# GpSimd's multiplies and adds of the even mixer and of three norms, moved to VectorE in a two-layer diffusion step

## The chip, the cores and the metric

The kernel runs on one core of one Trainium2 chip. Its time is the device time of one execution in microseconds (us). The engines are named as in the profile: PE is TensorE (matrix products), DVE is VectorE, ACT is ScalarE, POOL is GpSimd, SP issues the DMAs. Each engine works through a queue of its own in order, and an instruction at the head of a queue that waits for another engine holds up all behind it.

## The reference, cut to what matters

Two layers over 128 context and 512 latent tokens (640 columns in all), 1024 features. Layer 0 mixes with pooling and a short convolution, layer 1 with attention; each is followed by a SwiGLU block, and each of these sub-layers begins with an RMS norm.

```python
def rms_norm(x, g):
    return x * rsqrt(mean(x * x, -1) + EPS) * g
def window_mean(x, w):            # centred, w = 2, 4, 8, 16 for the four groups of 128 features
    return (cs[hi] - cs[lo]) / cnt
def pool_mixer(u, w_grp, scale):  # per group
    return einsum(window_mean(ug, w) - ug, w_grp) * scale
def short_conv_mixer(bg, cg, v, conv_w, conv_b):
    z = cg * v
    conv = sum(zp[:, k:k+L] * conv_w[k] for k in range(3)) + conv_b
    return bg * conv
def even_mixer(h, ...):
    u, bg, cg, v = split(h @ w_in)
    return concat([pool_mixer(u), short_conv_mixer(bg, cg, v)]) @ w_out
```

## The kernel before, in words

Activations lie transposed: 128 features on the partitions, the 640 tokens in the columns, so the 1024 features are eight blocks. All numbers are 32-bit. A product of two 32-bit matrices is made of three passes of PE: each operand is split into a high part (made by ACT, line 142) and the rest (a subtraction, line 143, on DVE). Names that begin with `wh`/`wl` are the two parts of a weight, `ah`/`al` and `bh`/`bl` those of an activation. A weight block of 128 output features takes 48 matmuls of 320 columns.

**The even mixer.** `project("pi", ...)` makes 16 blocks of the input product `pi`: four for pooling, then for each of four `j` the blocks c, v and b of the convolution. A block is taken out of PSUM by DVE (`ev`, line 505), and its shift column by ACT (line 510); three PSUM tiles go round, so PE can begin block n+3 only when block n has been taken out, and the small products `py` of the pooling take tiles from the same three. `pool_branch` builds the window sums by doubling: one add for width 2, two for 4, three for 8, four for 16, all on POOL (line 878). `conv_sum` multiplies c and v (line 935, POOL, after ACT has added the shift to c) and adds the two outer taps (line 958, POOL; ACT makes the scaled copies, line 957); for `j = 3` the same is done by DVE alone (lines 939 and 960). Then `project("po", ...)` makes the eight blocks of the output product.

**Beside it** DVE computes the modulation rows of both layers, which belong to no block: `ada.run` (line 365, `junk`) multiplies a 1024-wide row by the conditioning vector in halves of 512 with a sum. They are pinned into DVE's queue in program order, some in each block; between them a scheduler places the other instructions by its own estimates when the program is built, so the order in a queue is fixed before the run.

**The norms.** `updater` makes what follows each output block: the residual (three DVE instructions, line 490), `prep` (the next product's operand: `ah` by ACT, line 467, `al` by DVE, line 469) and `nrm.add`, the square by ACT (line 422) and its addition to the sum `ssq` by POOL (line 424, seven per norm). It serves three norms: `a1` after the even mixer, `b0` after layer 0's SwiGLU, `b1` after attention. `finish` splits the sum (lines 142 and 143) and PE adds it over the partitions (`ms`, line 453), one block into the next product `fi`.

Of the kernel before, what the change touches and what calls it, by code (L numbers as in the profile page):

```python
# [11 lines left out]
AF = mybir.ActivationFunctionType  # L12
ALU = mybir.AluOpType
# [4 lines left out]
KB = D // P  # L18
CTX = 128
LAT = 512  # L20
T = CTX + LAT
# [37 lines left out]
def hybrid_step(  # L59
# [23 lines left out]
    V, S, G, PE = nc.vector, nc.scalar, nc.gpsimd, nc.tensor  # L83
# [18 lines left out]
    def tmp(name):  # L102
        return tpool.tile([P, UL], F32, tag="t", name=name)

    x = pers.tile([P, KB, T], F32, name="x")
# [30 lines left out]
    def bias(ev, cond):  # L136
        return ev[:, T + cond : T + cond + 1]
# [8 lines left out]
    class Pipe:  # L146


        def __init__(self):
            self.due, self.now = [], 0  # L150
# [35 lines left out]
    class Stream:  # L186
# [7 lines left out]
        eng = V  # L194
# [213 lines left out]
    class Norm:  # L408
        def __init__(self, name):
            self.name = name  # L410
            self.acc = tmp(f"ssq_{name}")
            self.n = 0

        def add(self, k, eng=None, cols=slice(0, T), pool_only=False):
            if pool_only and k > 1:
# [13 lines left out]
    def log_exp_tables():  # L429
        tc.keep_in_program_order(S.preload_act_table_set("natural_log_exp_and_others"))  # L430
# [31 lines left out]
    def prep(k, dst, l, n):  # L462
        assert (l, 3 * n + 1, 4 if (l, 3 * n + 1, 4) in known and k < 4 else 8) in known
        h, lo = dst
        s = sc[l, n]
        for c, a, b in SEG:
            S.activation(h[:, k, a:b], x[:, k, a:b], AF.Identity, scale=s[:, k, c : c + 1])  # L467
        for c, a, b in SEG:
            V.scalar_tensor_tensor(  # L469
                out=lo[:, k, a:b],  # L470
                in0=x[:, k, a:b],
                scalar=s[:, k, c : c + 1],
                in1=h[:, k, a:b].bitcast(F32),
                op0=ALU.mult,
                op1=ALU.subtract,
            )

    def prep_shift(dst, l, n):
        assert (l, 3 * n, 8) in known
        h, lo = dst  # L480
        sh = mod[l][:, 24 * n : 24 * n + 8, :]
        V.tensor_copy(h[:, :, T:TX], sh)
        V.tensor_tensor(out=lo[:, :, T:TX], in0=sh, in1=h[:, :, T:TX].bitcast(F32), op=ALU.subtract)

    def update(m, l, gate0, parts):

        assert (l, gate0 // 8, 8) in known
        for c, a, b, got in parts:
            xs = x[:, m, a:b]
            V.scalar_tensor_tensor(  # L490
                out=xs,
                in0=got[:, 0 : b - a],
                scalar=mod[l][:, gate0 + m, c : c + 1],
                in1=xs,
                op0=ALU.mult,
                op1=ALU.add,
            )

    def residual(ps, m, l, gate0):
        parts = ((0, 0, CTX, ps[:, 0]), (1, CTX, HT, ps[:, 0, CTX:]), (1, HT, T, ps[:, 1]))  # L500
        update(m, l, gate0, parts)
# [11 lines left out]
    def shifted(ev):  # L513
        for c, a, b in SEG:
            S.activation(ev[:, a:b], ev[:, a:b], AF.Identity, bias=bias(ev, c))
        return ev
# [29 lines left out]
    def updater(l, gate0, nrm, then):  # L546
        def done(k, ps):
            residual(ps, k, l, gate0)
            prep(k, *then)
            nrm.add(k)  # L550
            if k == KB - 1:
                prep_shift(*then)
                log_exp_tables()
                pipe.later(1, lambda: [nrm.finish(span) for span in ((0, HT), (HT, T))])

        return done
# [167 lines left out]
    with tc.tile_pool(name="pool1", bufs=1) as p1:  # L724
# [41 lines left out]
        nrm = Norm("a0")  # L766
# [85 lines left out]
        def seqs(pad):  # L852
            return ((0, pad, CTX), (1, 2 * pad + CTX, LAT))
# [11 lines left out]
        def pool_branch(g, ev):  # L865
            up = tmp(f"up_{g}")
            for z in (0, PAD + CTX, 2 * PAD + T):
                G.memset(up[:, z : z + PAD], 0.0)
            for c, o, n in seqs(PAD):
                a = c * CTX  # L870
                S.activation(up[:, o : o + n], ev[:, a : a + n], AF.Identity, bias=bias(ev, c))
            w, cur, lo, hi = 1, up, 0, UL
            while w < WINDOWS[g]:
                nxt = tmp(f"s_{g}_{w}")
                q = w // 2
                lo, hi = (lo + 1, hi) if w == 1 else (lo + q, hi - q)
                back, on = (1, 0) if w == 1 else (q, q)
                G.tensor_tensor(
                    out=nxt[:, lo:hi], in0=cur[:, lo - back : hi - back], in1=cur[:, lo + on : hi + on], op=ALU.add
                )  # L880
                w, cur = 2 * w, nxt
            pipe.later(2, lambda: pool_mid(g, up, cur))

        def pool_mid(g, up, cur):
            pl = tmp(f"pl_{g}")
            for c, o, n in seqs(PAD):
                e = ends(cur, o, n, PAD)
                V.tensor_tensor(out=e, in0=e, in1=edge(g)[:, c], op=ALU.mult)
                V.scalar_tensor_tensor(
                    out=pl[:, c * CTX : c * CTX + n],  # L890
                    in0=cur[:, o : o + n],
                    scalar=1.0 / WINDOWS[g],
                    in1=up[:, o : o + n],
                    op0=ALU.mult,
                    op1=ALU.subtract,
                )
            plp = tuple(t[:, (5, 6, 4, 5)[g], 0:T] for t in bufB)
            pair(plp, pl[:, 0:T])
            pipe.later(3, lambda: pool_end(g, plp))
# [23 lines left out]
        ZL = T + 3  # L923

        def conv_sum(j, evc, evv):

            z = tmp(f"z_{j}")
            for o in (0, CTX + 1, ZL - 1):
                G.memset(z[:, o : o + 1], 0.0)
            if j < 3:  # L930
                shifted(evc)
            for c, o, n in seqs(1):
                a = c * CTX
                if j < 3:
                    G.tensor_tensor(
                        out=z[:, o : o + n], in0=evc[:, a : a + n], in1=evv[:, a : a + n], op=ALU.mult
                    )
                else:
                    V.scalar_tensor_tensor(
                        out=z[:, o : o + n],  # L940
                        in0=evc[:, a : a + n],
                        scalar=bias(evc, c),
                        in1=evv[:, a : a + n],
                        op0=ALU.add,
                        op1=ALU.mult,
                    )
            cvt = tmp(f"cv_{j}")

            def cw(i):
                return sm[:, S_CW + 4 * i + j : S_CW + 4 * i + j + 1]  # L950

            inner = slice(1, ZL - 1)
            S.activation(cvt[:, inner], z[:, inner], AF.Identity, scale=cw(1), bias=sm[:, S_CB + j : S_CB + j + 1])
            for i, d, t in ((0, -1, evc), (2, 1, evv)):
                zd = z[:, 1 + d : ZL - 1 + d]
                if j < 3:
                    S.activation(t[:, inner], zd, AF.Copy, scale=cw(i))
                    G.tensor_tensor(out=cvt[:, inner], in0=cvt[:, inner], in1=t[:, inner], op=ALU.add)
                else:
                    V.scalar_tensor_tensor(  # L960
                        out=cvt[:, inner], in0=zd, scalar=cw(i), in1=cvt[:, inner], op0=ALU.mult, op1=ALU.add
                    )
            return cvt

        def conv_gate(j, evb, cvt):
# [15 lines left out]
        def mixer_in(i, ev):  # L981
            if i < 4:
                return pool_branch(i, ev)
            j, what = divmod(i - 4, 3)
            if what == 0:
                evs["c"] = ev
            elif what == 1:
                evs["z"] = conv_sum(j, evs["c"], shifted(ev))
            else:
                cvt = evs["z"]  # L990
                if j < 3:
                    pipe.later(1, lambda: conv_gate(j, ev, cvt))
                else:
                    conv_gate(j, ev, cvt)
# [560 lines left out]
```

## Time and profile before

| | |
|---|---|
| time, median of 3 runs | 1409.69 us (1408.79 to 1410.60) |
| the profiled execution's own time | 1408.83 us |
| its span in the profile | 1406.9 us, 22549 instructions |
| PE, busy share of the span | 97% |
| DVE, busy share | 72% |
| ACT, busy share | 41% |
| POOL, busy share | 11% |
| mean granted PE clock | 0.983 of full speed |

The span runs from the first to the last instruction; the execution's own time holds 1.9 us more. The shares are averages over stages that differ: DVE is busy nine tenths or more in the slices from 70 to about 245 us, six to eight tenths of them from there to 600 us, and less on the whole after that. An instruction's duration counts its queueing for memory too, so the same form can be long in one place and short in another.

### The profile page before, as it was taken

The page shows a single profiled execution, that of the slowest core. Times are in us where ns is not written, and L with a number is a line of the kernel's source. Part 1 is how long each engine was busy: PE and PEld are TensorE (multiplying, and loading weights), DVE is VectorE, ACT ScalarE, POOL GpSimd, SP SyncE. Part 2 cuts the span into 40 slices and gives each one's busy share as a digit, 9 for nine tenths or more (in the row PEclk, how much of TensorE's full clock was granted, in tenths as well). Part 3 has the DMA queues.
Part 4 walks back from the last instruction along what each step waited for, and adds up shares of the span by engine and source line. Part 5 has one row for each costly group of instructions (what it writes and reads, how often), then busy time and mean ns, then how long its engine had stood idle before and what let it go on. Part 6 is the DMA issues. An engine that isn't in the chain of part 4 may idle for free.

```text
span 1406.9 us, 22549 instructions
## 1 busy us (share of the span) xinstructions
PE 1361.5 (97%) x9139; PEld 1332.9 (95%) x9139; DVE 1006.5 (72%) x1955; ACT 578.1 (41%) x1025; POOL 148.4 (11%) x116
## 2 busy tenths in 40 slices
PE   6989998999999999999999999999999999999995
PEld 3889998999999999999999899999999999999995
DVE  4899999777768787754667677778973477536745
ACT  3433334332112221232465676547652255414543
POOL 3351112000000000000203221020000000000003
PEclk7999999999999999999999999999999999999998
DMA  9634544434343534221232111012132122311212
GB/s 363 248 106 153 184 150 157 152 135 165 135 165 122 176 123 168 87 90 46 91 110 93 46 46 39 31 44 77 41 111 91 32 89 90 121 61 61 76 46 75
DMA packets 36728, 154.50 MB, mean 110 GB/s; under 512 B 3984, under 2 KB 11152, under 8 KB 26000
## 3 DMA queue, kind: packets, MB, share of 16 engines
q1 hardware_dynamic: 36624, 153.07, 31.2%
q8 instruction: 71, 1.16, 0.3%
q14 instruction: 33, 0.27, 0.1%
HBM read 147.55 MB, written 2.88 MB: 107 GB/s over the span
## 4 chain that ended last, share of the span: by engine, by line
PE 78%; DVE 16%; issue 2%; ACT 2%; DMA 1%; POOL 1%; SPq 0%; DVEq 0%; POOLq 0%; ACTq 0%
PE fi L287 26%; PE fo L287 21%; PE fi L610 16%; DVE junk L365 6%; PE pq L287 5%; PE wa L287 2%; DVE al L469 2%; PE o L1289 2%; PE s L1239 1%; DVE wl_in L143 1%; PE t L1272 1%; DVE x L490 1%; DVE wl_out L143 1%; DVE bl L143 1%; DMA raw_ada<-wada 1%
## 5 line engine op out<-in xcount | busy, mean ns | idle before, releaser
L365 DVE CUSTOM_DVE_ANT_0 junk<-rawa,silb 128x512 f32<-128x512 f32 x336 | 250.5, 746 | 7.6 <-ACT silb L793 1.0
L287 PE MATMUL fi<-al,wh_fi 128*128 128x320 f32 x832 | 192.2, 312 | 2.2 <-DVE al L469 2.2
L287 PE MATMUL fi<-ah,wh_fi 128*128 128x320 f32 x832 | 192.5, 313 | 1.4 <-ACT ah L467 1.4
L287 PE MATMUL fi<-ah,wl_fi 128*128 128x320 f32 x832 | 191.6, 312 | 0.0
L490 DVE SCALAR_TENSOR_TENSOR x<-fo,mod,x 128x128 f32<-128x128 f32 (+1 forms) x144 | 54.6, 433 | 136.5 <-PE fo L287 133.1
L287 PEld LDWEIGHTS fi<-al,wh_fi 128*128 128x128 f32 x832 | 141.7, 190 | 2.8 <-DVE al L469 2.8
L287 PEld LDWEIGHTS fi<-ah,wh_fi 128*128 128x128 f32 x832 | 141.7, 191 | 1.6 <-ACT ah L467 1.6
L287 PEld LDWEIGHTS fi<-ah,wl_fi 128*128 128x128 f32 x832 | 141.4, 190 | 0.0
L142 ACT ACTIVATE wh_fi<-raw_fi 128x1024 fp32r<-128x1024 f32 x52 | 55.0, 1058 | 172.0 <-PE fi L287 134.8
L142 ACT ACTIVATE wh_fi_p<-raw_fi 128x512 fp32r<-128x512 f32 x126 | 77.3, 627 | 111.8 <-PE fi L610 65.0
L142 ACT ACTIVATE wh_fo<-raw_fo 128x1024 fp32r<-128x1024 f32 (+1 forms) x48 | 47.5, 991 | 180.5 <-PE fo L287 132.6
L143 DVE TENSOR_TENSOR wl_fi_p<-raw_fi,wh_fi_p 128x512 fp32r<-128x512 f32 x126 | 85.6, 688 | 48.5 <-ACT wh_fi_p L142 48.2
L610 PE MATMUL fi<-bh,wl_fi_p 128*128 128x320 f32 x288 | 88.9, 309 | 0.0
L610 PE MATMUL fi<-bh,wh_fi_p 128*128 128x320 f32 x288 | 88.7, 308 | 0.0
L610 PE MATMUL fi<-bl,wh_fi_p 128*128 128x320 f32 x288 | 88.3, 307 | 0.0
L287 PE MATMUL fo<-bh,wh_fo 128*128 128x320 f32 x352 | 80.6, 310 | 0.0
L287 PE MATMUL fo<-bh,wl_fo 128*128 128x320 f32 x352 | 80.5, 310 | 0.0
L287 PE MATMUL fo<-bl,wh_fo 128*128 128x320 f32 x352 | 80.4, 310 | 0.0
L424 POOL TENSOR_TENSOR ssq_b<-ssq_b,sq_b 128x640 f32<-128x640 f32 x14 | 25.2, 1801 | 516.6 <-ACT sq_b L422 516.5
L287 PE MATMUL fo<-al,wh_fo 128*128 128x320 f32 x328 | 75.1, 310 | 0.0
L287 PE MATMUL fo<-ah,wh_fo 128*128 128x320 f32 x328 | 74.9, 309 | 0.0
L287 PE MATMUL fo<-ah,wl_fo 128*128 128x320 f32 x328 | 74.8, 309 | 0.0
(342 smaller groups left out, 3317.1 us busy)
## 6 DMA issues: line engine op xcount, KB each, us to landing
raw_fi<-wfi SPq DMA_DIRECT2D x44, 1024.0 KB, 4.8
rawa<-wada SPq DMA_DIRECT2D x84, 512.0 KB, 3.5
raw_fo<-wfo SPq DMA_DIRECT2D x16, 1024.0 KB, 4.9
raw_ada<-wada SPq DMA_DIRECT2D x12, 512.0 KB, 9.3
raw_in<-win SPq DMA_DIRECT2D x6, 1024.0 KB, 6.4
raw_fo<-wfo SPq DMA_DIRECT2D x8, 768.0 KB, 4.2
raw_qkv<-wqkv SPq DMA_DIRECT2D x6, 1024.0 KB, 4.8
raw_out<-wout SPq DMA_DIRECT2D x4, 1024.0 KB, 4.8
```

What stands on the lines that cost most here:

```text
L142: S.activation(h, src, AF.Copy)
L143: eng.tensor_tensor(out=l, in0=src, in1=h.bitcast(F32), op=ALU.subtract)
L287: PE.matmul(ps[:, h, 0 : hi - lo], w[a][:, k, cols], rhs[b][:, k0 + k, lo:hi], start=k == 0 and a == b, stop=k == kn - 1 and a == 1,)
L365: op = V.tensor_tensor_reduce(out=junk, in0=raw[:, cols], in1=silb[:, c, cols], scale=1.0, scalar=0.0, op0=ALU.mult, op1=ALU.add, accum_ou ...
L424: (eng or G).tensor_tensor(out=self.acc[:, cols], in0=self.acc[:, cols], in1=sq[:, cols], op=ALU.add)
L469: V.scalar_tensor_tensor(out=lo[:, k, a:b], in0=x[:, k, a:b], scalar=s[:, k, c : c + 1], in1=h[:, k, a:b].bitcast(F32), op0=ALU.mult, op1= ...
L490: V.scalar_tensor_tensor(out=xs, in0=got[:, 0 : b - a], scalar=mod[l][:, gate0 + m, c : c + 1], in1=xs, op0=ALU.mult, op1=ALU.add,)
L610: PE.matmul(out, w[a][:, k, :], ops.get(OPERAND[p], b)[:, k, :], start=fresh and k == 0 and a == b, stop=k == ops.kn - 1 and a == 1, skip_ ...
L1239: PE.matmul(self.ps[:, hf, 0:HT], bufB[a][:, self.h, q0 : q0 + P], kt[b][:, self.kv, hf * HT : hf * HT + HT], start=n == 0, stop=n == 2,)
L1272: PE.transpose(flat(pt)[:, s * P : s * P + P], self.pe[:, s * P : s * P + P], ident)
L1289: PE.matmul(po[:, 0 : 2 * P], vt[a][:, self.kv, s * P : s * P + P], got[b][:, s, :], start=s == 0 and n == 0, stop=s == 4 and n == 2,)
```

## The change

Every POOL multiply and add named above goes to DVE: the ten window sums; the three products c·v with the shift as the instruction's scalar operand, so that ACT's shift of c goes; the six outer taps as one multiply-add each, so that ACT's scaled copies go. `Norm` gets `square` and `add_square`: the square is made ahead of `prep`, and the addition is put behind `prep` and one block late, on DVE. `Norm.add` stays for the first and the last norm.

```diff
+        def square(self, k):
+            sq = tmp(f"sq_{self.name}_{k}") if k else self.acc
+            S.activation(sq[:, 0:T], x[:, k, :], AF.Square)
+            self.waiting.append(sq)
+
+        def add_square(self, eng):
+            sq = self.waiting.pop(0)
+            if sq is not self.acc:
+                eng.tensor_tensor(out=self.acc[:, 0:T], in0=self.acc[:, 0:T], in1=sq[:, 0:T], op=ALU.add)
...
             residual(ps, k, l, gate0)
+            nrm.square(k)
             prep(k, *then)
-            nrm.add(k)
+            if k:
+                nrm.add_square(V)
+            if k == KB - 1:
+                nrm.add_square(V)
...
-                G.tensor_tensor(
+                V.tensor_tensor(
                     out=nxt[:, lo:hi], in0=cur[:, lo - back : hi - back], in1=cur[:, lo + on : hi + on], op=ALU.add
                 )
...
-            if j < 3:
-                shifted(evc)
             for c, o, n in seqs(1):
                 a = c * CTX
-                if j < 3:
-                    G.tensor_tensor(
-                        out=z[:, o : o + n], in0=evc[:, a : a + n], in1=evv[:, a : a + n], op=ALU.mult
-                    )
-                else:
-                    V.scalar_tensor_tensor(
...
+                V.scalar_tensor_tensor(
+                    out=z[:, o : o + n],
+                    in0=evc[:, a : a + n],
+                    scalar=bias(evc, c),
+                    in1=evv[:, a : a + n],
+                    op0=ALU.add,
+                    op1=ALU.mult,
+                )
...
-                if j < 3:
-                    S.activation(t[:, inner], zd, AF.Copy, scale=cw(i))
-                    G.tensor_tensor(out=cvt[:, inner], in0=cvt[:, inner], in1=t[:, inner], op=ALU.add)
-                else:
-                    V.scalar_tensor_tensor(
...
+                V.scalar_tensor_tensor(
+                    out=cvt[:, inner],
+                    in0=z[:, 1 + d : ZL - 1 + d],
+                    scalar=cw(i),
+                    in1=cvt[:, inner],
+                    op0=ALU.mult,
+                    op1=ALU.add,
+                )
```

The scheduler orders the queues anew. The first place is DVE's queue where the pooling begins, from the first part of the weight split `wl_in_0_546` (`s` are window sums, `pl` the pooled result, `kc` the edge factors). Before:

```order
L143 TENSOR_TENSOR wl_in_0_546<-raw_in_138,wh_in_0_545 128x1024
L888 TENSOR_TENSOR s_1_556<-s_1_556,kc 128x2x8 x2
L143 TENSOR_TENSOR wl_in_1_675<-raw_in_138,wh_in_1_674 128x1024
L889 SCALAR_TENSOR_TENSOR pl_568<-s_1_556,up_550 128x128
L889 SCALAR_TENSOR_TENSOR pl_568<-s_1_556,up_550 128x512
L888 TENSOR_TENSOR s_2_566<-s_2_566,kc 128x2x8 x2
L143 TENSOR_TENSOR bl<-pl_568,bh 128x640
```

The same stretch of DVE's queue with the change:

```order
L143 TENSOR_TENSOR wl_in_0_546<-raw_in_138,wh_in_0_545 128x1024
L892 TENSOR_TENSOR s_1_556<-up_550 128x663
L143 TENSOR_TENSOR wl_in_1_675<-raw_in_138,wh_in_1_674 128x1024
L892 TENSOR_TENSOR s_1_564<-up_558 128x663
L902 TENSOR_TENSOR s_1_556<-s_1_556,kc 128x2x8 x2
L892 TENSOR_TENSOR s_2_566<-s_1_564 128x661
L903 SCALAR_TENSOR_TENSOR pl_568<-s_1_556,up_550 128x128
L903 SCALAR_TENSOR_TENSOR pl_568<-s_1_556,up_550 128x512
L902 TENSOR_TENSOR s_2_566<-s_2_566,kc 128x2x8 x2
L892 TENSOR_TENSOR s_1_581<-up_575 128x663
L143 TENSOR_TENSOR bl<-pl_568,bh 128x640
L892 TENSOR_TENSOR s_2_583<-s_1_581 128x661
```

The window sums (line 892) stand among the splits; up to the eviction `ev_751`, which frees the PSUM tile that PE asks for at 84.5 us, all ten of them and twelve `junk` halves (nine before) stand in the queue.

The second place is DVE's queue some twelve us later, at the weight part `wl_in_1` that PE needs for its next block. Before:

```order
L143 TENSOR_TENSOR bl<-pl_828,bh 128x640
L365 ISA junk,got_16_588<-rawa_593,silb 128x512
L365 ISA got_16_588 128x1
L143 TENSOR_TENSOR wl_in_1_856<-raw_in_678,wh_in_1_855 128x1024
```

With the change:

```order
L143 TENSOR_TENSOR bl<-pl_828,bh 128x640
L365 ISA junk,got_16_588<-rawa_593,silb 128x512
L365 ISA got_16_588 128x1
L945 SCALAR_TENSOR_TENSOR z_840<-ev_751,ev_835 128x128
L365 ISA junk,got_16_588<-rawa_599,silb 128x512
L365 ISA got_16_588 128x1
L945 SCALAR_TENSOR_TENSOR z_840<-ev_751,ev_835 128x512
L365 ISA junk,got_16_588<-rawa_599,silb 128x512
L365 ISA got_16_588 128x1
L143 TENSOR_TENSOR wl_in_1_852<-raw_in_678,wh_in_1_851 128x1024
```

The two products `z` and two more halves now stand ahead of that split; it is `wl_in_1_856` before and `wl_in_1_852` after.

The third place is the end of the first of the three norms, DVE's queue behind the residual of output block 6 (`sq_a_6` is its square). Before:

```order
L490 SCALAR_TENSOR_TENSOR x<-po_2011,mod_77,x 128x320
L469 SCALAR_TENSOR_TENSOR al<-x,sc_80,ah 128x128
L143 TENSOR_TENSOR wl_fi_0_1_2157<-raw_fi_0_1734,wh_fi_0_1_2156 128x1024
L469 SCALAR_TENSOR_TENSOR al<-x,sc_80,ah 128x512
L365 ISA junk,got_40_2018<-rawa_1880,silb 128x512
```

With the change:

```order
L500 SCALAR_TENSOR_TENSOR x<-po_1998,mod_77,x 128x320
L479 SCALAR_TENSOR_TENSOR al<-x,sc_80,ah 128x128
L365 ISA junk,got_40_2005<-rawa_1796,silb 128x512
L365 ISA got_40_2005 128x1
L422 TENSOR_TENSOR ssq_a_1578<-ssq_a_1578,sq_a_6_2063 128x640
L479 SCALAR_TENSOR_TENSOR al<-x,sc_80,ah 128x512
```

The addition of the square (line 422) has come between the two parts of `al`.

## Rows read from the trace of the kernel before

**Rows 1.** PE's waits: for whom, us in total, times, longest us.
```profile
PE pi L287 <- ACT ev L510: 5.8, 1, 5.8
...
PE pi L287 <- DVE wl_in L143: 5.3, 3, 2.5
...
PE fi L287 <- DVE al L469: 2.2, 2, 1.5
...
PE ms_a L453 <- ACT bh L142: 1.6, 1, 1.6
```

**Rows 2.** Windows: length, busy us (instructions) by engine, PE's clock, DMA share, GB/s.
```profile
84.00:100.00 16.00, 10.22 (x55) 9.96 (x54) 16.00 (x35) 6.75 (x12) 5.64 (x7) 0.79 0.28 94
100.00:160.00 60.00, 60.00 (x404) 59.80 (x403) 59.31 (x116) 21.74 (x35) 16.59 (x19) 1.00 0.49 164
160.00:170.00 10.00, 7.57 (x41) 7.31 (x40) 9.90 (x25) 2.80 (x4) 0.00 (x0) 0.83 0.54 194
230.00:250.00 20.00, 16.26 (x88) 15.22 (x87) 17.73 (x40) 9.73 (x17) 4.05 (x2) 0.83 0.48 167
670.00:710.00 40.00, 40.00 (x273) 40.00 (x272) 22.73 (x44) 20.14 (x31) 12.89 (x7) 1.00 0.32 112
926.00:957.00 31.00, 29.52 (x199) 29.10 (x199) 28.35 (x47) 19.58 (x33) 12.26 (x7) 1.00 0.19 69
```

**Rows 3.** Timeline at 100 us: start, us, engine, line, operation, out<-in, count.
```profile
99.91 1.22 DVE L143 TENSOR_TENSOR wl_in<-raw_in,wh_in 128x1024 fp32r<-128x1024 f32 x1
100.46 4.08 POOL L958 TENSOR_TENSOR cv<-cv,ev 128x641 f32<-128x641 f32 x2 [1.76 <-ACT ev L957]
101.05 2.06 DVE L365 CUSTOM_DVE_ANT_0 junk<-rawa,silb 128x512 f32<-128x512 f32 x1
101.18 0.56 PE L287 MATMUL pi<-ah,wl_in 128*128 128x320 f32 x2
```

**Rows 4.** DVE's groups by form, 64 to 101 us: count, busy us, mean ns, idle.
```profile
L365 DVE CUSTOM_DVE_ANT_0 junk<-rawa,silb 128x512 f32<-128x512 f32 x17 | 13.7, 805 | 0.0
L143 DVE TENSOR_TENSOR wl_in<-raw_in,wh_in 128x1024 fp32r<-128x1024 f32 x4 | 6.0, 1490 | 1.6 <-ACT wh_in L142 1.6
L889 DVE SCALAR_TENSOR_TENSOR pl<-s,up 128x128 f32<-128x128 f32 x4 | 4.7, 1162 | 0.0
...
L888 DVE TENSOR_TENSOR s<-s,kc 128x16 f32<-128x16 f32 x8 | 2.1, 303 | 2.4 <-POOL s L878 2.4
```

**Rows 5.** The same groups, 101 to 161 us.
```profile
L365 DVE CUSTOM_DVE_ANT_0 junk<-rawa,silb 128x512 f32<-128x512 f32 x46 | 40.1, 872 | 0.7
L143 DVE TENSOR_TENSOR wl_in<-raw_in,wh_in 128x1024 fp32r<-128x1024 f32 x8 | 11.1, 1386 | 0.0
L505 DVE TENSOR_TENSOR ev<-pi,rstd 128x640 f32<-128x640 f32 x7 | 5.7, 818 | 0.0
```

**Rows 6.** The same groups, 161 to 238 us.
```profile
L365 DVE CUSTOM_DVE_ANT_0 junk<-rawa,silb 128x512 f32<-128x512 f32 x48 | 36.7, 764 | 0.7
L143 DVE TENSOR_TENSOR wl_out<-raw_out,wh_out 128x1024 fp32r<-128x1024 f32 x8 | 15.2, 1903 | 0.0
```

**Rows 7.** The same groups, 260 to 600 us, where POOL has no instruction.
```profile
L365 DVE CUSTOM_DVE_ANT_0 junk<-rawa,silb 128x512 f32<-128x512 f32 x191 | 131.6, 689 | 4.4
L143 DVE TENSOR_TENSOR wl_fi<-raw_fi,wh_fi 128x1024 fp32r<-128x1024 f32 x32 | 39.1, 1223 | 0.0
...
L143 DVE TENSOR_TENSOR bl<-ea,bh 128x640 fp32r<-128x640 f32 x16 | 13.1, 820 | 0.0
```

**Rows 8.** Instructions on tile z by line: count, ns minimum/median/maximum, starts, forms.
```profile
L939 DVE SCALAR_TENSOR_TENSOR z<-ev,ev x2: 346/545/744, 173.5 to 173.7; 128x128 f32<-128x128 f32 x1, 128x512 f32<-128x512 f32 x1
L960 DVE SCALAR_TENSOR_TENSOR cv<-z,sm,cv x2: 882/883/884, 175.7 to 177.1; 128x641 f32<-128x641 f32 x2
```

**Rows 9.** DVE's timeline at the first weight split and the first late eviction.
```profile
63.66 1.23 DVE L143 TENSOR_TENSOR wl_in<-raw_in,wh_in 128x1024 fp32r<-128x1024 f32 x1 [1.55 <-ACT wh_in L142]
...
89.22 0.81 DVE L505 TENSOR_TENSOR ev<-pi,rstd 128x640 f32<-128x640 f32 x1
```

More of the change, by code (lines that the diff above doesn't have):

```diff
@@ L411, in __init__ @@
             self.acc = tmp(f"ssq_{name}")
-            self.n = 0
+            self.waiting = []
+        def square(self, k):
[6 more added lines that the diff above has]
+                eng.tensor_tensor(out=self.acc[:, 0:T], in0=self.acc[:, 0:T], in1=sq[:, 0:T], op=ALU.add)
         def add(self, k, eng=None, cols=slice(0, T), pool_only=False):
@@ L929, in conv_sum @@
                 G.memset(z[:, o : o + 1], 0.0)
-            if j < 3:
-                shifted(evc)
             for c, o, n in seqs(1):
                 a = c * CTX
-                if j < 3:
-                    G.tensor_tensor(
-                        out=z[:, o : o + n], in0=evc[:, a : a + n], in1=evv[:, a : a + n], op=ALU.mult
-                    )
-                else:
-                    V.scalar_tensor_tensor(
[L940 to L946, printed above, removed]
+                V.scalar_tensor_tensor(
[6 more added lines that the diff above has]
+                )
             cvt = tmp(f"cv_{j}")
@@ L953, in conv_sum @@
             S.activation(cvt[:, inner], z[:, inner], AF.Identity, scale=cw(1), bias=sm[:, S_CB + j : S_CB + j + 1])
-            for i, d, t in ((0, -1, evc), (2, 1, evv)):
-                zd = z[:, 1 + d : ZL - 1 + d]
-                if j < 3:
-                    S.activation(t[:, inner], zd, AF.Copy, scale=cw(i))
-                    G.tensor_tensor(out=cvt[:, inner], in0=cvt[:, inner], in1=t[:, inner], op=ALU.add)
-                else:
-                    V.scalar_tensor_tensor(
-                        out=cvt[:, inner], in0=zd, scalar=cw(i), in1=cvt[:, inner], op0=ALU.mult, op1=ALU.add
-                    )
+            for i, d in ((0, -1), (2, 1)):
+                V.scalar_tensor_tensor(
[6 more added lines that the diff above has]
+                )
             return cvt
```

## The prediction, made blind

> **What bounds the kernel now.** I read the page's busy shares first, then PE's waits, then windows around them, then DVE's groups by form. The share says PE, 97%; but a change on DVE and POOL can only win what PE loses, so its waits decide. Behind the start-up they lie in three places of the even mixer and one after attention. *A*, at 84.5 us: PE waits 5.8 us for the eviction of a `pi` block [rows 1]. *B*, in 160 to 170: PE is busy 7.57 of 10 us, and the wait is for a weight split `wl_in` [rows 1, 2]. *C*, in 230 to 250: PE is busy 16.26 of 20 us [rows 2], so 3.7 us of waits, 2.2 - 1.5 = 0.7 of it for `al` and 1.6 for the norm's sum [rows 1]. *E*, the 1.5 us wait for `al` at 955 us [rows 1].
>
> Each of A, B, C also drops PE's granted clock from its upper level (2.4 GHz) to its lower (1.2): its mean is 0.79 over 16 us at A, 0.83 over 10 at B, 0.83 over 20 at C [rows 2], so 16 x 0.21 = 3.4, 1.7 and 3.4 us of full-speed work are lost besides. PE loses 5.8 + 3.4 at A, 2.4 + 1.7 at B, 3.7 + 3.4 at C: 9.2 + 4.1 + 7.1 = 20.4 us. Between them PE never stops and DVE is busy 59.31 of 60 us [rows 2]. DVE's queue is thus the one that is late, and the question is whether it gets shorter or longer.
>
> **What POOL costs DVE today.** Look at one spot: a `junk` half that takes 689 ns where POOL is silent [rows 7] takes 2.06 us while POOL adds the taps [rows 3]. It is no single case: `junk` averages 805, 872 and 764 ns in the three parts of the stretch [rows 4 to 6]. Against the silent stretch (a split of 1024 columns 1223 ns, `junk` 689 [rows 7]; `pl` of 128 columns against the 346 of the `z` multiply [rows 8]) the excess is:
> - 64 to 101 us: 17 x 0.116 + 4 x 0.267 + 4 x 0.816 = 6.3 us, and 2.4 us of idle waiting for POOL's sums [rows 4]. Smaller forms are left out.
> - 101 to 161 us: 46 x 0.183 + 8 x 0.163 = 9.7 us [rows 5].
> - 161 to 238 us: 48 x 0.075 + 8 x 0.680 = 9.0 us [rows 6].
>
> Together 25.0 us of stretching and 2.4 of waiting. The evictions, whose one input is PSUM, are not stretched: 818 ns in the same window [rows 5], the length of the 640-column form elsewhere, 820 [rows 7].
>
> The Trainium skill ("SBUF — State Buffer", section "Who interferes with whom") has the rule: a DVE instruction with two SBUF inputs and a GpSimd one that reads SBUF exclude each other, and the second is blocked for the whole of the first; one with a single SBUF input is free. The rows agree on both kinds. To the letter, DVE would get back up to POOL's whole busy time, 16.59 us in 100 to 160 [rows 2], where the rows above show 9.7 of stretching; the sum would then be that of the first rival below.
>
> **What DVE takes on.** Ten window sums of 649 to 663 columns, by the 820 ns of 640 columns [rows 7] about 0.85: 8.5 us. Three products, 0.346 + 0.744 [rows 8]: 3.3. Six taps at 0.883 [rows 8]: 5.3. Seven additions for `a1` at 0.82: 5.7. That is 22.8 us in 29 instructions; successive ones overlap by 0.08 (a split of 1.22 begins at 99.91, the next instruction at 101.05 [rows 3]), so 20.5 us of queue. These durations come from the same forms, or one 3% narrower; bounds 0.74 and 0.95 for a window sum change the total by 1.1. So DVE's queue is lighter by 25.0 + 2.4 - 20.5 = 6.9 us at the least. ACT loses three shifts of c and six scaled copies; it is busy 21.74 of 60 us [rows 2], so that is worth nothing.
>
> **Place by place**, steps being durations less 0.08.
> *A.* The queue from the first split (63.66 [rows 9]) to the eviction that PE waits for now holds three splits (3.4), ten sums (7.7), three pairs of `pl` (2.8), edges (0.5), two `bl` (1.5), one eviction (0.7) and twelve `junk` (7.3): 23.9 us, so it starts at 87.6 instead of 89.22 [rows 9]. A shrinks by 1.6 us; the clock still drops. From there to `wl_in_1` stand ten more `junk` (6.1), two evictions (1.5), two `bl` (1.5), a `py` step (0.8), edges, `pl` and `z` (2.1): 12 us, it starts at 99.6 and ends at 100.8. PE, which reached that weight at 101.18 [rows 3], is there at 99.6 and now waits 1.2 us. Net 0.4.
> *B.* Until 161 us DVE loses 9.7 and takes on 6 x 0.80 + 2 x 0.94 = 6.7: it is 3.0 + 0.4 us ahead, more than the 2.4 of the wait. B goes with its clock loss: 4.1.
> *C.* Behind that, 9.0 are lost and 7 x 0.74 = 5.2 taken on: lead 7.2, of which PE has used 0.4 + 4.1; 2.7 of the 3.7 us of waits go. The rest, about 1 us, is less than E's wait of 1.5, and around that the granted clock stayed at 1.00 [rows 2]; so the 3.4 go too: 6.1. The last addition stands behind `al` and `sq`, and takes 0.82 in place of POOL's.
> *Norm b0.* In 670 to 710 PE never stops and DVE is busy 22.73 of 40 us [rows 2]; seven additions of 0.82 are hidden: nothing. *Norm b1.* The same seven are taken on where DVE is stretched too; E is the bound, 0 to 1.5, I take 0.7.
> Sum: 0.4 + 4.1 + 6.1 + 0.7 = 11.3 us. In part of the stretch DVE will have caught up with PE and idle, which wastes lead; I take 10.5. The profiled execution took 1408.83, so 1398.3; the runs' median is 0.9 higher: **1399 us**.
>
> **The rivals.**
> *All waits go, A too.* For it: the smaller forms, left out above, are stretched too (303 ns for 16 columns [rows 4]), and A's clock loss hangs on its length. Against: A's queue above, twelve `junk` among it. Then 20.4 + 0.7: 1389.
> *A new wait at `wl_in_1` drops the clock.* The split stands behind both `z` products now. If A does not shrink and the new wait is 2.5 us as at B, 1.7 to 3.4 us of clock go with it, and C keeps its drop: 1404 to 1406.
> *A wash.* Each moved instruction costs DVE as long as POOL's blocked it: 29 x 0.74 against 25 us, less lead lost to order. 1409. The Trainium skill says it of the pair ("Perfetto Trace Analysis", section "Optimizing Scalar/DVE Operations"): since the two share a read port, moving work between them might not help. The rows say a blocked `junk` loses 1.37 us (2.06 - 0.69), an added one costs 0.74, so not an even trade.
> *Slower.* The long instructions are long for another cause, such as the weight transfers landing meanwhile (DMA share 0.49 in 100 to 160 [rows 2]). Then 20.5 us join a queue that has no slack, less the 2.4 of idle: PE waits 18 more, 1428. It decides if `junk` keeps over 800 ns without POOL. Against: the long ones sit under POOL's spans [rows 3], and from 260 to 600 us weights land all the time while `junk` stays at 689 [rows 7].
>
> **How the numbers follow.** Forecast 0.60, all waits go 0.12, new wait 0.13, a wash 0.08, slower 0.07. A measurement of this kernel can tell 0.2% (2.8 us) from no change. The first three are faster; of the wash 0.02 is faster and 0.05 within; so faster 0.87, same 0.06, slower 0.07. The range reaches to most of the first two rivals: 1390 to 1405.
>
> **What would show it.** Right: `junk` near 690 ns in all of 64 to 240 us, no PE wait at 160 or behind the last `po` block, PE's clock at its upper level there, a wait of 4 to 5 us left at A and one of about 1 us at the second weight part behind it. Wrong: `junk` still over 800 ns; or short instructions, but an A as long as now, since the order of the queue sets it and not its sum; or a wait for the norm's sum behind the additions.

## The result, and the profile after

The changed kernel takes 1394.59 us (median; 1394.27 to 1395.23). The kernel before, run beside it, takes 1409.4 (1408.79 to 1410.6). The ratio is 0.9897, 95% interval 0.9886 to 0.9909: faster by 14.8 us, where the prediction took 10.5 off. The profiled span went from 1406.9 to 1392.5 us.

I read PE's waits first, as before the change. These are all of them from 60 to 260 us (for whom, us in total, times, longest us):

```profile
PE pi L287 <- ACT ev L520: 3.8, 1, 3.8
PE pi L287 <- DVE wl_in L143: 0.6, 1, 0.6
```

The 5.8 us of place A are 3.8, and the waits of B and C are gone [rows 1]. The same windows as before, for the clock:

```profile
84.00:100.00 16.00, 11.66 (x61) 11.14 (x60) 16.00 (x45) 6.09 (x11) 0.33 (x6) 0.79 0.40 129
100.00:160.00 60.00, 60.00 (x404) 60.00 (x405) 59.23 (x136) 18.48 (x31) 0.33 (x6) 1.00 0.52 185
160.00:170.00 10.00, 10.00 (x69) 10.00 (x68) 9.97 (x23) 3.51 (x5) 0.00 (x0) 1.00 0.58 210
230.00:250.00 20.00, 20.00 (x137) 20.00 (x136) 19.10 (x45) 9.01 (x18) 0.00 (x0) 1.00 0.53 183
926.00:957.00 31.00, 31.00 (x211) 31.00 (x210) 27.14 (x50) 21.55 (x36) 0.00 (x0) 1.00 0.30 103
```

In all four of these windows behind A, PE is busy all of the time and its granted clock is at the upper level; against [rows 2], 160 to 170 went from 7.57 to 10.00 busy us, 230 to 250 from 16.26 to 20.00, 926 to 957 from 29.52 to 31.00. In 100 to 160 DVE is as full as before (59.23 us for 59.31), but with 136 instructions for 116. Its groups by form show why, in 64 to 101 us:

```profile
L365 DVE CUSTOM_DVE_ANT_0 junk<-rawa,silb 128x512 f32<-128x512 f32 x23 | 16.0, 694 | 0.0
L143 DVE TENSOR_TENSOR wl_in<-raw_in,wh_in 128x1024 fp32r<-128x1024 f32 x4 | 4.9, 1225 | 1.5 <-ACT wh_in L142 1.5
L892 DVE TENSOR_TENSOR s<-up 128x663 f32<-128x663 f32 x4 | 3.4, 846 | 0.0
L143 DVE TENSOR_TENSOR bl<-pl,bh 128x640 fp32r<-128x640 f32 x4 | 3.3, 830 | 0.0
...
L902 DVE TENSOR_TENSOR s<-s,kc 128x16 f32<-128x16 f32 x8 | 1.0, 174 | 0.0
```

in 101 to 161 us:

```profile
L365 DVE CUSTOM_DVE_ANT_0 junk<-rawa,silb 128x512 f32<-128x512 f32 x44 | 30.2, 686 | 0.1
L143 DVE TENSOR_TENSOR wl_in<-raw_in,wh_in 128x1024 fp32r<-128x1024 f32 x8 | 9.8, 1223 | 0.0
...
L961 DVE SCALAR_TENSOR_TENSOR cv<-z,sm,cv 128x641 f32<-128x641 f32 x6 | 5.3, 883 | 0.0
```

and in 161 to 238 us:

```profile
L365 DVE CUSTOM_DVE_ANT_0 junk<-rawa,silb 128x512 f32<-128x512 f32 x48 | 33.0, 688 | 0.3
L143 DVE TENSOR_TENSOR wl_out<-raw_out,wh_out 128x1024 fp32r<-128x1024 f32 x7 | 8.6, 1222 | 0.0
L422 DVE TENSOR_TENSOR ssq_a<-ssq_a,sq_a 128x640 f32<-128x640 f32 x7 | 5.8, 824 | 0.0
...
L500 DVE SCALAR_TENSOR_TENSOR x<-po,mod,x 128x128 f32<-128x128 f32 x8 | 2.8, 349 | 3.9 <-PE po L287 3.9
```

`junk` went from 805, 872 and 764 ns [rows 4 to 6] to 694, 686 and 688, the 689 of the stretch in which POOL has no instruction [rows 7]; the `wl_out` splits from 1903 to 1222. In the last stretch DVE now waits 3.9 us for PE.

Where the saving accrues is read from the start of two products (instruction count; ns minimum/median/maximum, first and last start in us), with the change:

```profile
L287 PE MATMUL po<-bh,wh_out x128: 307/310/316, 165.5 to 221.4; 128*128 128x320 f32 x128
...
L287 PE MATMUL fo<-bh,wh_fo x352: 305/309/314, 336.9 to 691.5; 128*128 128x320 f32 x176
```

and before:

```profile
L287 PE MATMUL po<-bh,wh_out x128: 307/309/316, 170.9 to 226.9; 128*128 128x320 f32 x128
...
L287 PE MATMUL fo<-bh,wh_fo x352: 305/309/314, 349.7 to 704.4; 128*128 128x320 f32 x176
```

So 5.4 us are won up to the first `po` block (A and B), 7.4 more up to the first `fo` (C), and 1.6 more by the end (14.4 in all), of which 1.5 are the wait of E.

### The profile page after: what moved, and what is told of

It reads as the page before. It is cut to its first block, busy times and chain, and to the rows that moved or that the text cites. A ratio compares the mean times of both kernels' runs of the same rounds, so it can differ in the third digit from the quotient of the medians.

```text
span 1392.5 us, 22551 instructions
## 1 busy us (share of the span) xinstructions
PE 1355.6 (97%) x9139; PEld 1329.9 (96%) x9139; DVE 1000.9 (72%) x1998; ACT 571.7 (41%) x1013; POOL 69.9 (5%) x73
## 4 chain that ended last, share of the span: by engine, by line
PE 90%; DVE 7%; issue 1%; ACT 1%; DMA 1%; SPq 0%; POOL 0%; DVEq 0%; POOLq 0%; ACTq 0%
PE fi L287 27%; PE fo L287 22%; PE fi L624 16%; PE pq L287 5%; PE pi L287 5%; PE po L287 4%; PE wb L287 2%; PE wa L287 2%; DVE junk L365 2%; PE o L1295 2%; PE s L1245 1%; PE t L1278 1%; DMA raw_ada<-wada 1%; PE fo L1430 1%; DVE x L1415 1%
## 5 line engine op out<-in xcount | busy, mean ns | idle before, releaser
L365 DVE CUSTOM_DVE_ANT_0 junk<-rawa,silb 128x512 f32<-128x512 f32 x336 | 236.6, 704 | 6.6 <-ACT silb L807 1.0
L624 PE MATMUL fi<-xh,wh_fi_p 128*128 128x320 f32 x216 | 67.8, 319 | 0.1
```

Of the source, the lines that this page charges most:

```text
L365: op = V.tensor_tensor_reduce(out=junk, in0=raw[:, cols], in1=silb[:, c, cols], scale=1.0, scalar=0.0, op0=ALU.mult, op1=ALU.add, accum_ou ...
L624: PE.matmul(out, w[a][:, k, :], ops.get(OPERAND[p], b)[:, k, :], start=fresh and k == 0 and a == b, stop=k == ops.kn - 1 and a == 1, skip_ ...
```

## The experiments

The theory T is that of the prediction: a POOL operation with SBUF inputs holds up DVE's reads; without it DVE's queue is shorter, and PE's waits go where they were DVE's lateness. The rivals are that the time lay in the hand-offs between engines or in the order of the queues, and that each part is a wash. Ratios are to the kernel before, run on the same chip. A difference from the changed kernel is one between medians of separate rounds, in which the kernel before takes 1408.7 to 1409.4 us, so a difference of about 1 us says nothing.

### Each part undone by itself

**The window sums back on POOL.** In `pool_branch`:

```diff
-                V.tensor_tensor(
+                G.tensor_tensor(
```

> Only the ten window sums go back to POOL; conv and norms stay on DVE. Theory T (POOL's two-input operations hold up DVE's reads, so DVE's queue before PE's late eviction is as long as before the change): junk in 64 to 101 us is back near 800 ns and the splits there near 1.5 us, DVE waits some 2.4 us for the sums, PE's wait at 84 us grows from 3.8 to 5 to 6 us, nothing changes behind 160 us; 1396 to 1398 us. Rival R (the time was in the hand-offs between engines and in the order, not in the reads): junk keeps 690 ns and DVE, 8 us of work lighter, waits only for the hand-offs; PE's wait at 84 us shrinks; 1390 to 1393. Wash W: the sums cost DVE what POOL's cost it by blocking; 1394 to 1395.

Measured: 1398.02 us, ratio 0.9922 (0.9908 to 0.9935), 3.4 above the changed kernel (the intervals touch). DVE in 64 to 101 us:

```profile
L365 DVE CUSTOM_DVE_ANT_0 junk<-rawa,silb 128x512 f32<-128x512 f32 x19 | 15.0, 791 | 0.0
...
L902 DVE TENSOR_TENSOR s<-s,kc 128x16 f32<-128x16 f32 x8 | 2.1, 302 | 2.4 <-POOL s L892 2.4
```

and PE's waits from 60 to 260 us:

```profile
PE pi L287 <- ACT ev L520: 5.8, 1, 5.8
PE pi L287 <- DVE wl_in L143: 1.1, 1, 1.1
```

As T says: the long instructions and the 2.4 us of idle are back, A is 5.8 us again, and B and C stay away. The waits are 2.5 us longer than the changed kernel's (6.9 for 4.4), which leaves 0.9 of the 3.4 open.

**The conv back on POOL and ACT.** `conv_sum` as it was for j < 3:

```diff
+            if j < 3:
+                shifted(evc)
...
+                    G.tensor_tensor(
+                        out=z[:, o : o + n], in0=evc[:, a : a + n], in1=evv[:, a : a + n], op=ALU.mult
+                    )
...
+                    S.activation(t[:, inner], zd, AF.Copy, scale=cw(i))
+                    G.tensor_tensor(out=cvt[:, inner], in0=cvt[:, inner], in1=t[:, inner], op=ALU.add)
```

> Only the conv goes back: products and taps of j = 0 to 2 on POOL, shift and scaled copies on ACT. Theory T: in 101 to 161 us junk is back near 870 ns, DVE loses 9.7 us to stretching for 6.7 of work taken off, so it is 3 us later at 160 us; PE's wait there returns with 1.5 to 2.5 us and the drop of its clock with 1 to 2; 1397 to 1400 us. Rival R: junk stays at 690 ns, no wait at 160 us, 1393 to 1395. Wash W: DVE is stretched, but has that much slack by 160 us, and PE does not wait; 1394 to 1396.

Measured: 1396.73 us, ratio 0.9912 (0.9897 to 0.9928), 2.1 above the changed kernel; the intervals overlap, so the size rests on the trace. DVE in 101 to 161 us, then PE's waits from 60 to 260:

```profile
L365 DVE CUSTOM_DVE_ANT_0 junk<-rawa,silb 128x512 f32<-128x512 f32 x44 | 37.7, 856 | 0.6
```

```profile
PE pi L287 <- ACT ev L520: 3.8, 1, 3.8
PE po L287 <- DVE bl L143: 0.8, 1, 0.8
PE pi L287 <- DVE wl_in L143: 0.4, 1, 0.4
PE po L287 <- ACT bh L142: 0.3, 1, 0.3
```

The stretching is nearly all back (`junk` took 872 ns in [rows 5]), as T says, but the wait at 160 us, which I expected, is not: only 1.1 us of waits for the operand of the first `po` blocks, with the clock at 1.00. In that half the wash is right, and the time lies between the two forecasts. So B goes with either of the two parts alone. That DVE's queue gets enough lead from the window sums alone is argued from these waits and was not shown by itself.

**The norms' additions back on POOL.** In `updater`, for all three norms:

```diff
-            nrm.square(k)
             prep(k, *then)
-            if k:
-                nrm.add_square(V)
-            if k == KB - 1:
-                nrm.add_square(V)
+            nrm.add(k)
```

> Only the updater of the three norms goes back: the square behind the preparation, its addition at once and on POOL. Theory T: in 161 to 238 us the wl_out splits are back near 1.9 us, DVE loses 9 us for 5.2 of work taken off; with the lead that it has at 161 us PE waits 2 to 4 us behind the last po block and the clock drops there for 2 to 3.4 us; the 1.5 us at 955 us return too; 1399 to 1403 us. Rival R: the splits stay at 1.22 us, the waits stay away; 1393 to 1395. Wash W: stretched, but the lead of the earlier stages covers it, only 955 us returns; 1395 to 1396.

Measured: 1404.1 us, ratio 0.9964 (0.9951 to 0.9976), 9.5 above the changed kernel, a little more than expected. Windows, then DVE in 161 to 238 us:

```profile
170.00:230.00 60.00, 59.53 (x404) 59.27 (x402) 56.18 (x123) 21.17 (x31) 13.56 (x6) 1.00 0.41 141
230.00:250.00 20.00, 17.36 (x96) 16.45 (x97) 18.35 (x40) 11.18 (x19) 2.54 (x1) 0.83 0.38 132
926.00:957.00 31.00, 29.52 (x200) 29.24 (x199) 28.72 (x46) 20.15 (x35) 12.27 (x7) 1.00 0.25 85
```

```profile
L365 DVE CUSTOM_DVE_ANT_0 junk<-rawa,silb 128x512 f32<-128x512 f32 x46 | 35.3, 768 | 0.7
L143 DVE TENSOR_TENSOR wl_out<-raw_out,wh_out 128x1024 fp32r<-128x1024 f32 x7 | 14.0, 1998 | 0.0
```

C is back: 0.5 + 2.6 us of waits and, by the mean clock of the window, 20 x 0.17 = 3.4 of slower work; E is back with 1.5. Together 8.0 of the 9.5. In the profiled executions the first `po` block, which lies ahead of all of these additions, already starts 1.0 us later than in the changed kernel (166.5 against 165.5), so about 1 us of the rest isn't theirs. The three parts undone one by one cost 3.4 + 2.1 + 9.5 = 15.0 us, where the whole change gave 14.8; that these agree is partly chance, since B's 4 us come back in none of the three.

**The additions on DVE, but not delayed.** Square behind `prep`, addition at once:

```diff
-            if k:
-                nrm.add_square(V)
-            if k == KB - 1:
-                nrm.add_square(V)
+            nrm.add(k, V)
```

> The norms' additions stay on DVE, but the square is made behind the preparation and the addition stands at once behind it, not one block late. Theory T (what counts is that POOL does not read, not the order): no wait returns, 1394 to 1396 us. Rival R (the delay is what frees PE): DVE's queue stands at each addition until ACT has made the square, PE waits 1.5 us or more for al or the norm's sum behind the last po block, with a drop of the clock: 1397 to 1401.

Measured: 1395.58 us, ratio 0.9904 (0.989 to 0.9917), 1.0 us above the changed kernel, within the intervals. PE's waits from 60 to 260 us are the same two (3.8 and 0.6). The order of square and addition made no difference that can be told here; the engine did.

**One norm alone**: additions on POOL at their old place for the norm `b0` only.

```diff
-            nrm.square(k)
+            pool = nrm.name == "b0"
+            if not pool:
+                nrm.square(k)
             prep(k, *then)
+            if pool:
+                nrm.add(k)
...
```

> Of the three norms only the one after layer 0's SwiGLU goes back to the additions on POOL, at their old place; a1 and b1 stay on DVE. Theory T (DVE's loss counts only where PE waits for DVE, and from 670 to 710 us it does not): POOL busy 13 us there and DVE stretched, PE still never stops, 1394 to 1396 us, so that the 9.5 us of the run with all three norms on POOL belong to a1 and b1. Rival R (additions on POOL cost time wherever they stand): 1397 us or more.

Measured: 1395.2 us, ratio 0.9901 (0.9884 to 0.9917): no change, so the 9.5 us belong to `a1` and `b1`. One detail of the expectation was wrong: DVE was not stretched there (the wide `al` took 744 ns, 747 in the changed kernel). The window, then one addition in the timeline (start, us):

```profile
664.00:720.00 56.00, 56.00 (x380) 56.00 (x380) 31.84 (x61) 31.97 (x59) 12.17 (x7) 1.00 0.26 91
```

```profile
679.03 0.74 DVE L479 SCALAR_TENSOR_TENSOR al<-x,sc,ah 128x512 fp32r<-128x512 f32 x1
679.51 1.69 POOL L434 TENSOR_TENSOR ssq_b<-ssq_b,sq_b 128x640 f32<-128x640 f32 x1 [3.61 <-ACT sq_b L432]
...
682.15 1.13 DVE L500 SCALAR_TENSOR_TENSOR x<-fo,mod,x 128x128 f32<-128x128 f32 x3 [2.38 <-PE fo L287]
```

The addition begins 0.26 us before DVE's last `al` ends and then runs in the 2.38 us in which DVE waits for PE.

### The collision by itself

The strongest rival was that the long instructions had another cause. Four kernels add POOL work that nothing waits for to the changed kernel, for j = 0 to 2; the queues of the other engines stay as they are, row for row. A copy of one column ties the work to its place. The first has additions:

```diff
+            if j < 3:
+                G.tensor_copy(spare[:, 0:1], evv[:, 0:1])
+                for i in range(3):
+                    G.tensor_tensor(out=spare, in0=x[:, i, :], in1=rstd, op=ALU.add)
```

> The changed kernel, with nine more POOL instructions that nothing waits for: in the conv of j = 0 to 2 POOL adds two tiles of 640 columns, both in SBUF, into a spare tile, three times each. The order on DVE, ACT, PE and SP is that of the changed kernel, row for row. Theory T (such an addition holds up DVE's reads): junk in 101 to 161 us goes from 686 to 820 to 870 ns and the splits from 1223 to about 1390, DVE loses 8 to 10 us where it has no slack, PE waits again near 130 to 170 us and its clock drops once; 1400 to 1407 us. Rival R (the long instructions came from the hand-offs or the order): junk 690 ns, 1394 to 1396.

Measured: 1404.7 us, ratio 0.997 (0.9959 to 0.9982): nine useless additions cost 10.1 us. DVE's timeline at the first three (start, us), and POOL's:

```profile
96.62 1.66 DVE L946 SCALAR_TENSOR_TENSOR z<-ev,ev 128x128 f32<-128x128 f32 x1
98.19 0.68 DVE L366 CUSTOM_DVE_ANT_0 junk<-rawa,silb 128x512 f32<-128x512 f32 x1
...
98.80 2.03 DVE L946 SCALAR_TENSOR_TENSOR z<-ev,ev 128x512 f32<-128x512 f32 x1
100.75 2.02 DVE L366 CUSTOM_DVE_ANT_0 junk<-rawa,silb 128x512 f32<-128x512 f32 x1
...
102.70 1.21 DVE L144 TENSOR_TENSOR wl_in<-raw_in,wh_in 128x1024 fp32r<-128x1024 f32 x1
```

```profile
96.21 6.01 POOL L957 TENSOR_TENSOR spare<-x,rstd 128x640 f32<-128x640 f32 x3
```

Three additions lengthen three DVE instructions by 1.3 us each (1.66 against 0.35 us for this form of `z` [rows 8], 2.03 against 0.74, 2.02 against 0.69); the `junk` between the two `z` and the split behind them have their own length. The engines take turns: a DVE instruction stands while an addition runs, then the next addition stands while a DVE instruction runs, which is why POOL's three show 6.01 us, 1.87 to 2.08 each; at 15 us of the kernel before, where DVE is idle, such an addition takes 1.53. The split `wl_in` ends late, PE waits for it here and once more, and its clock falls both times:

```profile
100.00:130.00 30.00, 24.93 (x156) 24.67 (x156) 28.71 (x54) 7.42 (x12) 8.10 (x12) 0.94 0.39 141
130.00:160.00 30.00, 28.80 (x184) 28.80 (x185) 29.30 (x56) 7.41 (x12) 7.03 (x7) 0.94 0.39 141
```

The expected figures for `junk` and the splits were off, since of the nine lengthened instructions six are `z` and three `junk` (`junk` 772 ns in 94 to 165 us), and the splits kept 1217 ns; the time came as T says, and the loss with nine times some 1.3 us is a little above it.

**POOL only writes**: six fills in place of the three additions.

```diff
+                for i in range(6):
+                    G.memset(spare, 0.0)
```

> As the kernel with the idle additions, but POOL only writes: six fills of 640 columns for each j, 18 in all, some 0.65 us each by the 524 ns of 512 columns, so about 12 us of POOL's time in the same places. Theory T (the reads are what collides): junk stays at 690 ns, no wait returns, 1394 to 1396 us. Rival R2 (any POOL instruction on SBUF slows DVE): junk above 780 ns, 1398 us or more.

Measured: 1395.19 us, ratio 0.9903 (0.9887 to 0.992). DVE and POOL in the same place:

```profile
96.91 0.35 DVE L946 SCALAR_TENSOR_TENSOR z<-ev,ev 128x128 f32<-128x128 f32 x1
97.17 0.68 DVE L366 CUSTOM_DVE_ANT_0 junk<-rawa,silb 128x512 f32<-128x512 f32 x1
```

```profile
96.48 4.09 POOL L957 MEMSET spare<- 128x640 f32 x6
```

POOL fills for 4.09 us beside them, and nothing is lengthened, here or at the other two `j` (`junk` 686 ns, `z` 350 and 750 in 94 to 165 us).

**POOL reads one tile**: three copies.

```diff
+                for i in range(3):
+                    G.tensor_copy(spare, x[:, i, :])
```

> As the kernel with the idle additions, but POOL reads one tile: three copies of 640 columns for each j, nine in all. Theory T as the prediction's page words it (any POOL instruction that reads SBUF counts): DVE loses as much for each us of POOL's time as with the additions, junk 800 ns or more, 1398 to 1406 us. Rival T2 (only a POOL instruction with two SBUF inputs collides): junk 690 ns, 1394 to 1396.

Measured: 1397.69 us, ratio 0.9919 (0.9904 to 0.9934), 3.1 above the changed kernel:

```profile
96.93 0.81 DVE L946 SCALAR_TENSOR_TENSOR z<-ev,ev 128x128 f32<-128x128 f32 x1
...
98.27 1.19 DVE L946 SCALAR_TENSOR_TENSOR z<-ev,ev 128x512 f32<-128x512 f32 x1
99.38 1.20 DVE L366 CUSTOM_DVE_ANT_0 junk<-rawa,silb 128x512 f32<-128x512 f32 x1
```

T2 falls: a copy collides too. But it lengthens the DVE instruction by 0.45 to 0.5 us, not by 1.3. My wording, as much for each us of POOL's time, fell as well: the three copies show 1.06 to 1.26 us, so DVE lost some 0.4 us for each us shown, with the additions some 0.65. POOL's shown time has its own waiting in it, and more than that.

**The additions cut in halves** of 320 columns:

```diff
+                for i in range(6):
+                    h = slice(i % 2 * HT, i % 2 * HT + HT)
+                    G.tensor_tensor(out=spare[:, h], in0=x[:, i // 2, h], in1=rstd[:, h], op=ALU.add)
```

> The kernel with the idle additions, but each addition of 640 columns is cut in two of 320: 18 for j = 0 to 2, the same columns in all. With nine of 640 POOL's additions and DVE's instructions took turns: POOL's took 1.92 us, 1.25 of it its own, and the DVE instruction behind it stood about 1.3 us. Theory T1 (a DVE instruction stands for the whole of one POOL instruction, by its own length): 18 times about 0.65 us, the same loss in all; DVE's long instructions are about 0.65 us long in excess and twice as many; 1402 to 1406 us. Rival R1 (a fixed price of 1.3 us for each collision): twice the loss; 1412 us or more. Rival R3 (short ones slip into the gaps between DVE's reads): 1396 to 1400.

Measured: 1402.33 us, ratio 0.9952 (0.9937 to 0.9967). The time can't be used: the second halves are not tied by the one-column copy, and all nine ran at 58.76 to 69.3 us, ahead of POOL's fills of `up`; DVE waited 3.8 us for these, and A grew to 7.8. The nine that stayed tell the price. DVE's groups by form from 94 to 165 us:

```profile
L946 DVE SCALAR_TENSOR_TENSOR z<-ev,ev 128x128 f32<-128x128 f32 x3 | 2.9, 956 | 0.0
```

0.61 us of excess for each (346 ns in [rows 8]), half of 1.3: the standing goes with the length of POOL's instruction and is no fixed price. It is some 0.25 us less than POOL's instruction takes where DVE is idle: 0.87 for the half additions at 66 to 69 us of this run, 1.53 for the whole one (the 1.25 of the expectation is a product of one tile with itself).

### A version that beats both

In the changed kernel PE still waits 3.8 us at A, for the eviction behind DVE's modulation rows, and its clock drops behind that. Dealing the rows out later:

```diff
-            each=lambda i: ada.run(1 + (i < 7) - (i >= 11)),
+            each=lambda i: ada.run((0, 1, 2, 2, 2, 2, 2, 2, 1, 1, 1, 1, 0)[i]),
```

> A version meant to be better: the modulation rows that DVE computes beside the 13 blocks of the input product are dealt out 0,1,2,2,2,2,2,2,1,1,1,1,0 in place of 2,2,2,2,2,2,2,1,1,1,1,0,0, so three rows of two halves, 4 us, leave the queue ahead of the eviction that PE waits 3.8 us for at 84 us. Theory T (that wait is DVE's queue and nothing else): the wait goes to 0 to 1.5 us and the drop of the clock behind it (3.4 us) with it; DVE has the rows to do later, where it is ahead; 1387 to 1390 us. Rival R (the slack behind is too small): a wait of 1.5 to 4 us and a drop of the clock come up between 100 and 230 us instead; 1392 to 1397.

Measured: 1389.92 us, ratio 0.9864 (0.985 to 0.9879), 4.7 below the changed kernel, with an interval that doesn't touch its own.

```profile
84.00:100.00 16.00, 14.98 (x99) 14.46 (x98) 15.74 (x36) 6.06 (x11) 0.16 (x3) 1.00 0.38 130
```

```profile
L287 PE MATMUL po<-bh,wh_out x128: 307/310/316, 160.0 to 215.9; 128*128 128x320 f32 x128
```

A's wait is gone and the clock stays up; 1.0 us for `wl_in` is left, and no wait comes up later, up to 260 us. The first `po` block begins 5.5 us earlier than in the changed kernel. A row has four `junk` halves, not two as the expectation said: 7 halves (16 for 23), 4.8 us, left the stretch from 64 to 101 us.

## Why the prediction was right, point by point

- **That DVE's queue is the late one, and POOL what lengthens it**: right, and shown from both sides. Undoing a part brings the length back, and additions that nobody needs do it in an unchanged order, while fills don't. The rival that the weights' landing made the instructions long is out: with a DMA share of 0.52 in 100 to 160, `junk` takes 686 ns.
- **What DVE takes on**: 0.85 us for a window sum was 846 ns, 0.883 for a tap 883, 0.82 for an addition 824.
- **A**, net 0.4 us: about 1.2. PE gets on at the second weight part at 99.94 us instead of 101.18 [rows 3]; 0.2 of this it has already ahead of A. The wait shrank by 2.0, not 1.6 (the eviction starts at 86.91), and the new wait at `wl_in_1` is 0.57 instead of 1.2. The clock drops as said, but its price of 3.4 us was a wrong reading: 16 x 0.21 counts the low clock also while PE stands. By the matmuls it is less. One takes 0.149 us at the upper level (60.00 us for 404 in 100 to 160); the 55 in 84 to 100 before took 10.22 busy us [rows 2], 2.0 more than at that pace, and the 61 with the change 11.66, 2.6 more. Since the term stood on both sides, it did not move the forecast; the 9.2 us that PE was said to lose at A were 7.8.
- **B**, 4.1 us: all gone, as said; PE's lead of 1.2 us is 5.4 at the first `po` block, so 4.2. The step's reason, 3 us won on the conv, was too narrow: B stays away also with the conv back on POOL.
- **C**, 6.1 us: 7.4. The step that failed in size is DVE's lead, put at 7.2 us, of which 2.7 were to be left for C's 3.7 us of waits, with 1 us of wait over. PE does not stop there, although it comes 5.4 us earlier, and DVE even waits 3.9 us for PE in 161 to 238.
- **Norm b0**, nothing: right, by the run with this norm alone on POOL. **Norm b1**, 0.7 of 0 to 1.5: the whole 1.5.
- **The 0.8 us taken off for wasted lead**: DVE did catch up with PE, but no wait of PE came of it, so nothing had to be taken off.

From these starts the terms are 1.2 + 4.2 + 7.4 + 1.6 = 14.4 us, the difference of the spans, against 11.3 in the sum and 10.5 in the forecast. A, C and E all erred to the same side: each was put too low. A part of the lead that the sum missed lies in the forms that the prediction left out of the stretching. In 64 to 101 us the edge products went from 303 ns [rows 4] to 174, 8 x 0.13 = 1.0 us; the four wide `pl` from 949 to 694, 1.0; and the splits `bl` to 830 from 1087, 1.0, in this row of before:

```profile
L143 DVE TENSOR_TENSOR bl<-pl,bh 128x640 fp32r<-128x640 f32 x4 | 4.3, 1087 | 0.0
```

That these 3 us are what covered C's remainder is worked out from rows and was not tried. Of the signs that the prediction named, `junk` near 690 ns, no wait at 160 us or behind the last `po` block and the clock there came out; A's wait of 3.8 us lies just below the 4 to 5 named.

On the rule of the Trainium skill that the prediction weighed ("SBUF — State Buffer", section "Who interferes with whom": a DVE instruction with two SBUF inputs and a GpSimd one that reads SBUF exclude each other for the whole instruction, one that only writes is free): the runs agree, with 1.3 us for each addition, 0.45 to 0.5 for each copy and nothing for the fills. The prediction's reading to the letter, POOL's whole busy time of 16.59 us as the loss, does not hold; its sum went by the 9.7 of the rows. An addition that shows 1.9 to 2.1 us beside DVE takes 1.53 where DVE is idle, and held DVE up for 1.3.

The Trainium skill's doubt ("Perfetto Trace Analysis", section "Optimizing Scalar/DVE Operations"), that moving work between the two might not help, is not borne out here: 1.3 us of standing went for 0.74 to 0.85 of work.

## What to carry to other kernels

An instruction that takes longer in one place than the same form elsewhere is the sign to look for: set it beside the other engine's timeline, and price the move as the standing that goes against the work that comes. Here a 640-column addition on POOL cost a busy DVE 1.3 us, and 0.74 when DVE did it itself; where DVE waits for PE anyway, the addition on POOL cost nothing. A few us of DVE work in front of an eviction cost twice over at A, in the wait and in PE's clock behind it, so look for work without a deadline there (the modulation rows) and deal it out later.

## What was not expected of the hardware

POOL stands as well: the one-column copy ahead of the idle additions took 0.69 us at 95.44, while DVE made a split `bl` from two SBUF tiles (0.82 us from 95.27), and 0.18 at 122.87, beside a `bl` of which one input is in PSUM. A tile that is tied to its place by one column ties only the instructions that touch this column: nine half additions ran 40 us and more early and delayed POOL's next useful work.
